# Turned blocks in fixed order, row power ahead of the weighted product, later transposes: one transformer block on one core

## The chip, the cores and the metric

The kernel runs on one core of a Trainium2 chip. A core has five engines that run side by side, each through its own queue in program order, and wait for each other through semaphores: TensorE (PE in the profile; its weight loads are PEld), VectorE (DVE), ScalarE (ACT), GpSimd (POOL) and SyncE (SP), which here only starts transfers. SBUF is the working memory of 128 partitions; PSUM holds what PE writes, in banks of 512 float32 per partition. The metric is the device time of one execution, in microseconds; lower is better.

## The reference

One block of depth 1 over 256 tokens of width 2048, all in float32: a feed-forward part, a mixer of two branches, and a second feed-forward part, each added to the running rows h after a norm of its own.

```python
def _rmsnorm(x, g):
    y = xf * lax.rsqrt(jnp.mean(xf * xf, axis=-1, keepdims=True) + NORM_EPS)
    return (y * g.astype(jnp.float32)).astype(x.dtype)

def _swiglu(x, w_gate, w_up, w_down):
    return (jax.nn.silu(x @ w_gate) * (x @ w_up)) @ w_down
...
f = _swiglu(_rmsnorm(h, ln_ffn1_pre[l]), ffn1_gate[l], ffn1_up[l], ffn1_down[l])
h = h + MACARON_WEIGHT * _rmsnorm(f, ln_ffn1_post[l])
mx = _hybrid_mixer(_rmsnorm(h, ln_mix_pre[l]), w_in[l], ...)
h = h + _rmsnorm(mx, ln_mix_post[l])
f = _swiglu(_rmsnorm(h, ln_ffn2_pre[l]), ffn2_gate[l], ffn2_up[l], ffn2_down[l])
h = h + MACARON_WEIGHT * _rmsnorm(f, ln_ffn2_post[l])
```

The hidden width of the feed-forward parts is 5632. The mixer projects to 8480 columns, runs a recurrence over 16 heads and a pooling branch, and ends with a 2048 x 2048 product. The change does not touch the mixer's inside.

## The kernel before

**Products in three.** Each float32 operand is cut in two: a rounded part (H, by a copy to the type fp32r) and what is left (L, by a subtraction). A product is three matmuls, H by H, H by L and L by H (`mm3`, lines 155 to 157; `mm` is the PSUM tile). Weights come as tiles of two k-steps of 128 rows by 512 columns (`get_w`, line 117, on SP's queue, into `w32`, four buffers). `two` casts a tile on ACT (line 131, `wH`, here called the cast) and subtracts on DVE (line 132, `wL`, the split); these pairs have five buffers. The 256 tokens are two halves, h = 0 and 1, of 128; a k-step of one half is three matmuls of 128x512.

**Turned blocks.** A product needs its left operand with the columns on the partitions. `transpose_split` (line 335) takes 128 tokens by 512 columns: PE transposes four pieces of 128x128 into one PSUM bank (line 339, tile `tr`). Where a norm stands ahead, its weights `gT` are multiplied in on the way: for each piece ACT writes scaled `xH` (line 345, the copy) and DVE scaled piece less `xH` (line 346, `xL`, the difference). These four pairs are called a block. The norm's other factor, one over the root of the row's mean square, is applied later, when the product leaves PSUM (`rs`).

**The head.** `head` writes the order of the first product by hand. x and the first gate weights are loaded in chunks, blocks are turned and tiles split, and PE runs k-steps of both halves as they come. `load(0, 0)` starts the first chunk of x on SP's queue; `load(None, None)` starts the norm weights' 16 rows of 128 (tile `g1rows`) and has PE turn and DVE copy them to `g1`. After the head, `stats` sums the squares of the rows (line 372, ACT, tile `junk`).

**The end of each part.** `post` multiplies by the down weights, 512 columns at a time (c = 0 to 3). For each half and c, when the product leaves PSUM, `sumsq` on ACT adds the squares (line 372, `ss`), and DVE multiplies the product by the post-norm weights (line 420, `fg`, here the product with the norm weights). At c = 2 the first three sums are gathered. After c = 3, `norm` makes the mean on DVE (line 439, tile `rt2`) and its power of -1/2 on POOL (line 441, the row power `r`); then `out` makes four row products on DVE (line 445: `fg` times `r` plus the residual), and `emit` stores each 512 columns on POOL's queue and has them turned for the next part. The last `post` stores the result through SP's queue instead and turns nothing.

**The order around the hand-over.** `run` keeps a clock of its own, `s.now`, in planned microseconds: items (k-steps of 3 x 0.2265) advance it, and events are recorded when it has reached their time. The last product (c = 3) runs its last 16 k-steps half by half (`by_half`): first all of half 0, then half 1. The next product begins by half too (`lead`, 10 k-steps of half 0, then 10 of half 1). When half h ends at `end`, the mean and power are recorded at `end` + 0.9, the four row products at `end` + 1.7, 2.4, 3.1 and 3.8, and the four turned blocks at `end` + `TURNS[h][q]` (line 44). Each turned block advances the clock by 0.45 (`TT`). So the blocks of half 0 stand among the last k-steps of half 1, and those of half 1 among the first k-steps of the next product. Two such hand-overs exist: from the first feed-forward part to the mixer, and from the mixer to the second feed-forward part. Casts and splits of the next product's tiles are events as well, 6.0 ahead of their k-steps (`AHEAD`). Within these stretches the order of PE, ACT and DVE is as recorded; elsewhere a scheduler of the framework orders the instructions by a plan of its own.

Of the kernel before, what the change touches and what calls it, by code (L numbers as in the profile page):

```python
# [14 lines left out]
ALU = mybir.AluOpType  # L15
# [25 lines left out]
STAG = 10  # L41
TRAIL = 16
AHEAD = (5.0, 6.0)
TURNS = [[3.6, 4.7, 5.8, 6.9], [3.6, 4.6, 5.6, 6.6]]
TB = 4

ROWS = [("ln_mix_pre", 16), ("ln_ffn2_pre", 16), ("mu", 26), ("w0", 8), ("a0", 8),
# [4 lines left out]
class Block:  # L52
# [154 lines left out]
    def head(s, w, c0, KT, do, keep, xs):  # L207

        load, turn = xs
        w32 = {}  # L210

        def get(k, n):
            w32[k] = (n, s.get_w(w, k, n, c0, 512, own=True))

        def split(k):
            n, t = w32[k]
            keep(s.two(t, k, n, 512))
        E = mybir.EngineType
        with s.tc.manual_schedule(engines={E.PE, E.Activation, E.DVE, E.SP}):
            load(0, 0)  # L220
            load(None, None)
            get(0, 1)
            get(1, 1)
            load(1, 0)
            get(2, 1)
            get(3, 1)
            for c in range(1, 4):
                load(0, c)
                get(4 * c, 2)
                load(1, c)  # L230
                get(4 * c + 2, 2)
            split(0)
            turn(0, 0)
            split(1)
            do(0, 0)
            turn(1, 0)
            split(2)
            do(1, 0)
            split(3)
            do(0, 1)  # L240
            do(1, 1)
            do(2, 0)
            do(2, 1)
            for c in range(4):
                k = 4 * c
                if c < 3:
                    turn(0, c + 1)
                    split(k + 4)
                if c:
                    for i in range(3):  # L250
                        do(k + i, 0)
                        do(k + i, 1)
                        if c < 3 and i == 1:
                            turn(1, c + 1)
                            split(k + 6)
                elif c < 3:
                    turn(1, c + 1)
                    split(k + 6)
                do(k + 3, 0)
                do(k + 3, 1)  # L260
            s.stats()
# [73 lines left out]
    def transpose_split(s, src, T, j, h, gT=None):  # L335
        nc = s.nc
        ps = s.psum("tr").rearrange("p (k t) -> p k t", k=4)
        for i in range(4):
            nc.tensor.transpose(ps[:, i], src[:, i * P:(i + 1) * P], s.ident)  # L339
        dH = T[j][0][:, :, h * P:h * P + P]  # L340
        dL = T[j][1][:, :, h * P:h * P + P]
        if gT is not None:
            for i in range(4):
                g = gT[:, j * 4 + i:j * 4 + i + 1]
                nc.scalar.activation(out=dH[:, i], in_=ps[:, i], func=AF.Copy, scale=g)  # L345
                nc.vector.scalar_tensor_tensor(out=dL[:, i], in0=ps[:, i], scalar=g,  # L346
                                               in1=dH[:, i].bitcast(F32), op0=ALU.mult,
                                               op1=ALU.subtract)
            return
        nc.scalar.copy(dH, ps)  # L350
        nc.vector.tensor_tensor(out=dL, in0=ps, in1=dH.bitcast(F32), op=ALU.subtract)

    def turn(s, T1, h, src):

        s.nc.vector.transpose(out=T1[:, h * 512:h * 512 + 512], in_=src)
# [46 lines left out]
    def post(s, wd, at, KT, gpost, fac, resid, emit, reload):  # L402
        nc = s.nc
        gb = [s.unit(p="gb") for _ in range(2)]
        fg = [[s.unit(p="fg") for _ in range(2)] for _ in range(2)]
        ss = [s.small(4, "ss") for _ in range(2)]

        def cc_(u, c):
            return u[c // 2][:, (c % 2) * 512:(c % 2) * 512 + 512]

        part = [None, None]
        kf = 1.0 / (D * fac ** 2)

        for c in range(4):
            def ev(h, ps):
                if h == 0 and c % 2 == 0:
                    nc.gpsimd.dma_start(out=gb[c // 2], in_=gpost[c * 512:c * 512 + 1024]  # L417
                                        .partition_broadcast(P))
                s.sumsq(ps, ss[h][:, c:c + 1])
                nc.vector.tensor_tensor(out=cc_(fg[h], c), in0=ps, in1=cc_(gb, c), op=ALU.mult)  # L420
                if c == 2 and h == 0:
                    reload()
                if c == 2:
                    p = s.small(1, "rt", bufs=2)
                    nc.vector.tensor_reduce(out=p, in_=ss[h][:, :3], axis=AX.X, op=ALU.add)
                    part[h] = s.small(1, "rp", bufs=2)
                    nc.vector.tensor_scalar(out=part[h], in0=p, scalar1=kf,
                                            scalar2=NORM_EPS / fac ** 2, op0=ALU.mult,
                                            op1=ALU.add)
                if c == 3:  # L430
                    end = s.now
                    r = s.small(1, "rs", bufs=8)
                    s.at(end + 0.9, lambda: norm(h, r))
                    for q in range(4):
                        s.at(end + 1.7 + 0.7 * q, lambda q=q: out(h, q, r, end))

            def norm(h, r):
                r2 = s.small(1, "rt2", bufs=2)
                nc.vector.tensor_scalar(out=r2, in0=ss[h][:, 3:4], scalar1=kf,
                                        scalar2=part[h], op0=ALU.mult, op1=ALU.add)  # L440
                nc.gpsimd.tensor_tensor(out=r, in0=r2, in1=s.mhalf[:, :1], op=ALU.pow)

            def out(h, q, r, end):
                o = cc_(fg[h], q)
                nc.vector.scalar_tensor_tensor(out=o, in0=o, scalar=r, in1=resid(h, q),  # L445
                                               op0=ALU.mult, op1=ALU.add)
                emit(h, q, o, end + TURNS[h][q])
            s.gemm_tok(wd, c * 512, at, KT, ev, trail=(c == 3))

    def next_pre(s, gT):  # L450
# [758 lines left out]
```

## Time and profile before

| | |
|---|---|
| median of 3 runs | 2136.59 us (2135.99 to 2136.96) |
| the profiled execution | 2136.39 us |
| its span, first to last instruction | 2134.7 us |
| mean granted TensorE clock | 0.993 |
| weights by SP's queue | 385.21 MB of 406.99 MB |
| mean rate of all transfers | 191 GB/s |

A span is what the profile covers; the time of an execution is a little longer. In rows of the profile an engine's name is followed by line, operation, the tile written, an arrow, and the tiles read. Sums count one of the engines alone; "[0.99 <-DVE fg]" behind a row is the time that the engine had idled just before, and what ended that idling. A matmul's duration includes its way through the array: those that follow each other start closer than a duration. PEclk is the share of the full clock that TensorE was granted.

### The profile page before, as it was taken

The page shows a single profiled execution, that of the slowest core. Times are in us where ns is not written, and L with a number is a line of the kernel's source. Part 1 is how long each engine was busy: PE and PEld are TensorE (multiplying, and loading weights), DVE is VectorE, ACT ScalarE, POOL GpSimd, SP SyncE. Part 2 cuts the span into 40 slices and gives each one's busy share as a digit, 9 for nine tenths or more (in the row PEclk, how much of TensorE's full clock was granted, in tenths as well). Part 3 has the DMA queues.
Part 4 walks back from the last instruction along what each step waited for, and adds up shares of the span by engine and source line. Part 5 has one row for each costly group of instructions (what it writes and reads, how often), then busy time and mean ns, then how long its engine had stood idle before and what let it go on. Part 6 is the DMA issues. An engine that isn't in the chain of part 4 may idle for free.

```text
span 2134.7 us, 28779 instructions
## 1 busy us (share of the span) xinstructions
PE 2099.6 (98%) x11077; PEld 1763.6 (83%) x11077; DVE 1261.6 (59%) x1588; ACT 1119.9 (52%) x1600; POOL 73.7 (3%) x161
## 2 busy tenths in 40 slices
PE   8999999999999999999999999989999999999998
PEld 6888888888888779989988788868888888888886
DVE  5555555565444465698789666565555555554444
ACT  6556555655444355465465444465665556554442
POOL 0000000000000000000210110000000000000000
PEclk9999999999999999999999999999999999999999
DMA  5665666667666556656546575556666665775654
GB/s 202 205 195 178 206 197 191 184 201 253 196 192 193 177 168 193 177 160 194 143 148 188 158 257 181 194 169 201 193 185 201 196 191 177 221 244 193 195 192 136
DMA packets 224116, 406.99 MB, mean 191 GB/s; under 512 B 13151, under 2 KB 49129, under 8 KB 223977
## 3 DMA queue, kind: packets, MB, share of 16 engines
q1 hardware_dynamic: 218089, 385.21, 58.7%
q0 software_dynamic: 5888, 19.93, 2.6%
q8 instruction: 87, 1.43, 0.3%
q14 instruction: 52, 0.43, 0.1%
HBM read 396.69 MB, written 8.39 MB: 190 GB/s over the span
## 4 chain that ended last, share of the span: by engine, by line
PE 95%; issue 2%; DVE 1%; ACT 1%; DMA 0%; POOL 0%; SPq 0%; DVEq 0%; POOLq 0%; ACTq 0%
PE mm L155 27%; PE mm L156 27%; PE mm L157 27%; PE mc L311 10%; PE tr L339 1%; DVE xL L346 0%; ACT xH L345 0%; PE pA L930 0%; ACT wH L131 0%; DVE wL L132 0%; PE pU L1026 0%; DVE fg L445 0%; PE pSa L1038 0%; PE pY L1061 0%; PE pY L1057 0%
## 5 line engine op out<-in xcount | busy, mean ns | idle before, releaser
L132 DVE TENSOR_TENSOR wL<-w,wH 128x1024 fp32r<-128x1024 f32 (+2 forms) x725 | 872.7, 1211 | 741.2 <-ACT wH L131 739.6
L131 ACT CAST wH<-w 128x1024 fp32r<-128x1024 f32 (+2 forms) x725 | 750.8, 1043 | 815.3 <-PE mm L157 673.0
L155 PE MATMUL mm<-wH,xH 128*128 128x512 f32 x2460 | 966.6, 393 | 8.3 <-ACT wH L131 7.8
L156 PE MATMUL mm<-wL,xH 128*128 128x512 f32 x2460 | 962.0, 391 | 5.7 <-DVE wL L132 5.7
L157 PE MATMUL mm<-wH,xL 128*128 128x512 f32 x2460 | 960.2, 391 | 0.0
L155 PEld LDWEIGHTS mm<-wH,xH 128*128 128x128 f32 x2460 | 463.8, 189 | 108.2 <-ACT wH L131 11.5
L156 PEld LDWEIGHTS mm<-wL,xH 128*128 128x128 f32 x2460 | 463.9, 189 | 103.1 <-DVE wL L132 8.8
L157 PEld LDWEIGHTS mm<-wH,xL 128*128 128x128 f32 x2460 | 463.8, 189 | 96.6
L311 PE MATMUL mc<-xH,wH 128*128 128x256 f32 x560 | 159.6, 285 | 0.0
L311 PE MATMUL mc<-xL,wH 128*128 128x256 f32 x560 | 158.4, 283 | 0.0
L311 PE MATMUL mc<-xH,wL 128*128 128x256 f32 x560 | 158.4, 283 | 0.0
L365 ACT COPY x<-T 32x256 f32<-32x256 f32 x352 | 141.9, 403 | 3.9
L311 PEld LDWEIGHTS mc<-xH,wH 128*128 128x128 f32 x560 | 105.9, 189 | 1.0
L311 PEld LDWEIGHTS mc<-xH,wL 128*128 128x128 f32 x560 | 106.0, 189 | 0.3
L311 PEld LDWEIGHTS mc<-xL,wH 128*128 128x128 f32 x560 | 106.0, 189 | 0.2
L345 ACT ACTIVATE xH<-tr,cols 128x128 fp32r<-128x128 f32 x64 | 22.6, 366 | 41.7 <-DVE xL L346 25.2
L384 ACT ACTIVATE sg<-mm,rs 128x512 f32<-128x512 f32 x44 | 30.1, 689 | 21.9 <-PE mm L157 21.9
L385 DVE SCALAR_TENSOR_TENSOR sg<-mm,rs,sg 128x512 f32<-128x512 f32 x44 | 31.7, 751 | 9.0 <-ACT sg L384 9.0
L372 ACT ACTIVATE junk<-mm 128x512 bf16<-128x512 f32 x24 | 14.3, 597 | 37.5 <-PE mm L157 37.5
L346 DVE SCALAR_TENSOR_TENSOR xL<-tr,cols,xH 128x128 fp32r<-128x128 f32 x64 | 22.0, 349 | 20.1 <-ACT xH L345 20.1
L417 POOL DMA_DIRECT2D gb<-in_ln_ffn_post_dram x4 | 2.4, 592 | 877.4 <-DVE xL L369 844.0
L420 DVE TENSOR_TENSOR fg<-mm,gb 128x512 f32<-128x512 f32 x24 | 16.5, 692 | 27.2 <-ACT junk L372 27.2
(243 smaller groups left out, 1110.4 us busy)
## 6 DMA issues: line engine op xcount, KB each, us to landing
w<-in_ffn_up_dram SPq DMA_DIRECT2D x176, 512.0 KB
w<-in_ffn_down_dram SPq DMA_DIRECT2D x176, 512.0 KB
w<-in_ffn_gate_dram SPq DMA_DIRECT2D x174, 512.0 KB
w<-in_w_in_dram SPq DMA_DIRECT2D x128, 512.0 KB
w<-in_w_out_dram SPq DMA_DIRECT2D x32, 512.0 KB
w<-in_w_proj_b_dram SPq DMA_DIRECT2D x16, 512.0 KB
w<-in_w_proj_a_dram SPq DMA_DIRECT2D x16, 512.0 KB
hsp<-fg POOLq DMA_DIRECT2D x16, 256.0 KB, 3.0
```

The lines of the kernel that those rows point to most:

```text
L131: s.nc.scalar.copy(vH, v)
L132: s.nc.vector.tensor_tensor(out=vL, in0=v, in1=vH.bitcast(F32), op=ALU.subtract)
L155: nc.tensor.matmul(ps, aH, bH, start=start, stop=False)
L156: nc.tensor.matmul(ps, aH, bL, start=False, stop=False)
L157: nc.tensor.matmul(ps, aL, bH, start=False, stop=stop)
L311: s.nc.tensor.matmul(o, lh, rh, start=one and n == 0, stop=k == KT - 1 and n == 2, skip_group_check=True)
L339: nc.tensor.transpose(ps[:, i], src[:, i * P:(i + 1) * P], s.ident)
L345: nc.scalar.activation(out=dH[:, i], in_=ps[:, i], func=AF.Copy, scale=g)
L346: nc.vector.scalar_tensor_tensor(out=dL[:, i], in0=ps[:, i], scalar=g, in1=dH[:, i].bitcast(F32), op0=ALU.mult, op1=ALU.subtract)
L365: nc.scalar.copy(dst[q * 32:q * 32 + 32, :, :, i], src[i * 32:i * 32 + 32, :, :, q])
L384: nc.scalar.activation(out=sg, in_=ps, func=AF.Sigmoid, scale=rs[h])
L385: nc.vector.scalar_tensor_tensor(out=sg, in0=ps, scalar=rs[h], in1=sg, op0=ALU.mult, op1=ALU.mult)
```

## The change

Four edits. In `transpose_split` the four copies of a block are recorded first and then the four differences. In `post` the product with the norm weights of c = 3 is recorded with the mean and the power, behind both. `TURNS` has later times. In the head, the transfer of the norm weights' rows is started ahead of the first chunk of x.

```diff
-TURNS = [[3.6, 4.7, 5.8, 6.9], [3.6, 4.6, 5.6, 6.6]]
+TURNS = [[4.2, 5.3, 6.4, 7.5], [4.0, 5.0, 6.2, 7.4]]
...
+            load(None, None)
             load(0, 0)
-            load(None, None)
             get(0, 1)
...
         if gT is not None:
-            for i in range(4):
-                g = gT[:, j * 4 + i:j * 4 + i + 1]
+            gs = [gT[:, j * 4 + i:j * 4 + i + 1] for i in range(4)]
+            for i, g in enumerate(gs):
                 nc.scalar.activation(out=dH[:, i], in_=ps[:, i], func=AF.Copy, scale=g)
+            for i, g in enumerate(gs):
                 nc.vector.scalar_tensor_tensor(out=dL[:, i], in0=ps[:, i], scalar=g,
                                                in1=dH[:, i].bitcast(F32), op0=ALU.mult,
                                                op1=ALU.subtract)
...
+                def scale():
+                    nc.vector.tensor_tensor(out=cc_(fg[h], c), in0=ps, in1=cc_(gb, c),
+                                            op=ALU.mult)
                 s.sumsq(ps, ss[h][:, c:c + 1])
-                nc.vector.tensor_tensor(out=cc_(fg[h], c), in0=ps, in1=cc_(gb, c), op=ALU.mult)
+                if c < 3:
+                    scale()
...
                     r = s.small(1, "rs", bufs=8)
-                    s.at(end + 0.9, lambda: norm(h, r))
+                    s.at(end + 0.9, lambda: (norm(h, r), scale()))
```

## The prediction

> **What bounds the kernel now.** I read the page first, then PE's waits, then windows around each wait, then the timelines in them. The page's busy times:
>
> ```profile
> PE 2099.6 (98%) x11077; PEld 1763.6 (83%) x11077; DVE 1261.6 (59%) x1588; ACT 1119.9 (52%) x1600; POOL 73.7 (3%) x161
> ```
>
> PE is busy nearly always, so only its waits, and time in which it runs slowly, can be won. The view of PE's waits (total us, times, longest) names whom it waits for:
>
> ```profile
> PE mm L155 <- ACT wH L131: 7.8, 9, 1.7
> PE tr L339 <- DVE fg L445: 5.8, 4, 1.9
> PE mm L156 <- DVE wL L132: 5.7, 8, 0.8
> ```
>
> By the timeline these sit in three stretches: the head, and the two hand-overs (down product to mixer, output product to second feed-forward). Windows (stretch, its length, busy us of PE, PEld, DVE, ACT, POOL with counts, PEclk, DMA share, GB/s):
>
> ```profile
> 17.05:42.24 25.19, 19.60 (x79) 14.00 (x77) 14.38 (x28) 14.14 (x30) 0.00 (x0) 0.93 0.35 130
> 42.24:66.00 23.76, 23.76 (x105) 19.64 (x106) 16.00 (x19) 18.14 (x30) 3.49 (x4) 1.00 0.75 230
> 734.71:763.75 29.04, 22.39 (x94) 16.61 (x93) 18.18 (x36) 13.39 (x31) 4.39 (x8) 0.82 0.48 159
> 1385.36:1414.74 29.38, 22.48 (x94) 16.97 (x92) 18.19 (x37) 13.73 (x32) 4.40 (x8) 0.83 0.48 162
> ```
>
> The second row is the undisturbed state: 105 matmuls in 23.76 us, 0.226 us each, clock 1.00. The other three have PE idle for 5.6 to 6.9 us, and a lower clock besides. What holds ACT and DVE there are the turned blocks:
>
> ```profile
> L345 ACT ACTIVATE xH<-tr,cols 128x128 fp32r<-128x128 f32 x64 | 22.6, 366 | 41.7 <-DVE xL L346 25.2
> L346 DVE SCALAR_TENSOR_TENSOR xL<-tr,cols,xH 128x128 fp32r<-128x128 f32 x64 | 22.0, 349 | 20.1 <-ACT xH L345 20.1
> ```
>
> Each copy waits for the difference before it, each difference for its copy. One period of the head (start, us, engine):
>
> ```profile
> 22.48 1.03 ACT L131 CAST wH<-w 128x1024 fp32r<-128x1024 f32 x1
> 23.41 0.37 ACT L345 ACTIVATE xH<-tr,g 128x128 fp32r<-128x128 f32 x1
> 23.55 1.22 DVE L132 TENSOR_TENSOR wL<-w,wH 128x1024 fp32r<-128x1024 f32 x1 [0.58 <-ACT wH L131]
> 25.07 0.37 ACT L345 ACTIVATE xH<-tr,g 128x128 fp32r<-128x128 f32 x1 [1.28 <-DVE xL L346]
> 25.86 0.37 ACT L345 ACTIVATE xH<-tr,g 128x128 fp32r<-128x128 f32 x1 [0.42 <-DVE xL L346]
> 26.91 1.04 ACT L131 CAST wH<-w 128x1024 fp32r<-128x1024 f32 x1
> ```
>
> Copies follow each other at 0.79 us, and cast to cast is 4.43 us. In that time PE has two k-steps for both halves (12 matmuls, 2.7 us) and one group of four transposes.
>
> **The change part by part.** *Copies, then differences.* The order of the built program shows that copies two to four of a block carry no wait, and differences two to four none; the first difference waits for the fourth copy. What such pieces take unhindered:
>
> ```profile
> 737.70 0.62 ACT L345 ACTIVATE xH<-tr,cols 128x128 fp32r<-128x128 f32 x2 [0.42 <-DVE xL L346]
> 770.31 0.60 DVE L346 SCALAR_TENSOR_TENSOR xL<-tr,cols,xH 128x128 fp32r<-128x128 f32 x2
> 40.20 3.88 ACT L131 CAST wH<-w 128x1024 fp32r<-128x1024 f32 x4
> 41.27 4.63 DVE L132 TENSOR_TENSOR wL<-w,wH 128x1024 fp32r<-128x1024 f32 x4 [0.58 <-ACT wH L131]
> 24.38 0.39 PE L157 MATMUL mm<-wH,xL 128*128 128x512 f32 x1
> 24.62 0.60 PE L339 MATMUL tr<-ident,x 128*128 128x128 f32 x4
> 25.28 0.39 PE L156 MATMUL mm<-wL,xH 128*128 128x512 f32 x1
> ```
>
> Two copies take 0.62, so one follows the other at 0.25 (0.62 less 0.37): four hold ACT for 1.02 and are done after 1.13. Differences: 0.26, four hold DVE 1.04. Casts follow at 0.95 (3.88 less 1.04, by three), splits at 1.13. A group of transposes adds 0.45 to PE (24.38 to 25.28 is 0.90, less two matmuls). A period then needs 1.97 of ACT, 2.17 of DVE, but 2.71 + 0.45 = 3.16 of PE: PE becomes the bound.
>
> *The first difference waits for the fourth copy.* That is the one lengthened wait: it comes 0.75 later than now, and the splits stand behind it on DVE. The sum contains it. The Trainium skill (PSUM — Partial Sum Buffer, PSUM bank collisions raise a hardware error) says that two engines must not touch one bank of the same partitions at a time, reads included, which agrees with the 25.2 us above; without that rule the first difference could follow the first copy, and the two hand-overs would gain up to 0.8 each more.
>
> *Head.* Early on, two waits of PE go, since the second tile's cast and split now finish by 7.5 and 8.3, ahead of PE:
>
> ```profile
> 8.85 0.79 PE L155 MATMUL mm<-wH,xH 128*128 128x512 f32 x1 [0.21 <-ACT wH L131]
> 9.57 0.29 PEld L156 LDWEIGHTS mm<-wL,xH 128*128 128x128 f32 x1 [0.44 <-DVE wL L132]
> 14.79 1.03 PE L339 MATMUL tr<-ident,x 128*128 128x128 f32 x8
> ```
>
> So what follows comes 0.65 sooner: the eight transposes at 14.1, the next four at 16.4 in place of 17.05. From there to 42.24, PE has k-steps 4 to 13 and the first matmul of the next, 61 matmuls, and four groups of transposes: 61 x 0.226 + 4 x 0.45 = 15.6. One wait is left: the copies of the block begin at 14.75 (0.63 after its transposes, as at the hand-over below), the last is done at 15.9, differences to 16.95, split to 18.2; PE, at 17.1 by then, waits 1.1. Later splits run ahead (2.17 against 3.16). Before 25.19, after 15.6 + 1.1 = 16.7, and 0.65 ahead: **-9.1**. The eight sums of squares follow among the next product's casts as now: 8 x 0.6 + 8 x 0.95 = 12.4 us of ACT against 96 matmuls, 21.7 us.
>
> *Norm rows' transfer first.* Row and wait:
>
> ```profile
> 1.25 0.42 SPq L1134 DMA_DIRECT2D g1rows<-in_ln_ffn_pre_dram  x1
> 7.52 0.71 PEld L339 LDWEIGHTS tr<-ident,x 128*128 128x128 f32 x4 [0.79 <-DMA x<-in_x_dram]
> ```
>
> The first chunk of x is issued 0.45 later, the weight tile behind both when it was. The chain passes the cast of that tile, and PE then waits 0.79 for the other half's chunk, which covers a shift. Bounds 0 to +0.45; I take 0, as the wait is the longer.
>
> *Turns later.* The planner's new times put each group of the first half one k-step (0.68) later, and spread those of the second half to one per k-step; the number of transposes is the same, so PE pays nothing. All four row products now stand ahead of the first differences on DVE. The rows of the first hand-over:
>
> ```profile
> 734.71 0.60 PE L339 MATMUL tr<-ident,fg 128*128 128x128 f32 x4
> 735.34 0.37 ACT L345 ACTIVATE xH<-tr,cols 128x128 fp32r<-128x128 f32 x1 [3.83 <-PE tr L339]
> 752.94 0.60 ACT L372 ACTIVATE junk<-mm 128x512 bf16<-128x512 f32 x1
> 756.88 1.12 PE L339 MATMUL tr<-ident,fg 128*128 128x128 f32 x4 [1.92 <-DVE fg L445]
> ```
>
> New times: groups at 735.39 and every 1.13 (0.68 + 0.45) to 738.78; six k-steps end the half at 743.3, six of the next product end at 747.4. ACT starts copies at 736.02 (0.63 after the transposes) and has, by the built order, four blocks and five casts ahead of the sum of squares: 4 x 1.02 + 5 x 0.95 = 8.8, so that starts at 744.85 in place of 752.94 and ends at 745.55. DVE starts differences at 737.15; four blocks and five splits, 4 x 1.04 + 5 x 1.13 = 9.8, to 747.0. Then the row power; what is late next is this, behind the splits. Its price is read at the end of the span, where nothing covers it:
>
> ```profile
> 2126.93 0.69 DVE L420 TENSOR_TENSOR fg<-mm,gb 128x512 f32<-128x512 f32 x1 [6.65 <-ACT junk L372]
> 2127.54 0.20 DVE L439 TENSOR_SCALAR rt<-ss,rp 128x1 f32<-128x1 f32 x1
> 2128.41 2.74 DVE L445 SCALAR_TENSOR_TENSOR fg<-fg,rs,h 128x512 f32<-128x512 f32 x4 [0.66 <-POOL rs L441]
> ```
>
> From the mean to the first row product 0.87, that product 0.75: transposes of the second half at 748.7, PE idle for 1.3. Four groups with a k-step each, 4.5, and the second half starts at 753.2. Before: 763.75. **-10.5**. The second hand-over has the same queues, 650.65 later: 1403.85 against 1414.74, **-10.9**. Nothing gives it back soon after: the second half's first differences are done by 750.8, for 753.2; four sums of squares (0.6 each) and the cast ahead of k-step 10 end by 757.1, its split by 758.8, for 760.0; DMA there moves 159 GB/s, against 230 in the undisturbed row.
>
> *Row power first.* The product with the norm weights (0.61 to the next row) leaves the chain, and is covered by the mean and the power (0.87). At the end of the span **-0.6** (0 if the cover fails); elsewhere it is in the times above. The new wait, the mean's for the sum of squares, is the product's old one, with the same work queued behind.
>
> **Sum.** 9.1 + 10.5 + 10.9 + 0.6 = 31.1 us. The profiled execution took 2136.39, 1.69 over its span of 2134.7, and lies 0.2 under the median: 2136.59 - 31.1 = **2105.5**.
>
> **Rivals.** *The slow clock stays.* Windows of 3.41 us:
>
> ```profile
> 17.11:20.52 3.41, 1.16 (x7) 0.61 (x6) 2.10 (x4) 1.83 (x4) 0.00 (x0) 1.00 1.05 386
> 20.52:23.93 3.41, 3.41 (x9) 2.64 (x10) 1.52 (x5) 2.30 (x5) 0.00 (x0) 0.50 1.05 386
> 737.32:740.73 3.41, 2.42 (x15) 1.80 (x14) 2.10 (x6) 1.36 (x4) 0.54 (x1) 1.00 0.16 59
> 747.56:750.97 3.41, 1.43 (x5) 0.86 (x5) 1.73 (x5) 1.86 (x4) 0.00 (x0) 1.00 0.53 146
> 750.97:761.21 10.24, 7.62 (x22) 5.62 (x23) 7.76 (x13) 4.38 (x10) 2.23 (x4) 0.50 0.68 227
> ```
>
> PE busy for 1.16 or 1.43 us of a window: half clock in the next. Busy for 2.42: none. My idles of 1.1 to 1.3 leave 2.1 to 2.3, nearer the latter. If they count, one window at half costs 1.7 us at three places, and 10.24 costs 5.1 at each hand-over: 2110.6 to 2117. The Trainium skill (TensorE: Matmul & The Clock Gate, Part 1: The HAM clock gate) gives a window of 3413 ns and half clock after an idle one; the lengths agree, but by its word an idle window would be needed and this rival would cost nothing, while here windows with 1.16 and 1.43 of work sufficed.
>
> *A wait for the fifth weight tile.* Four are buffered; the fifth is issued when the first is split, at 739.4, and cast, by my queue, at 743.9. If it lands 3 us later than that, beside the stores of the rows, the row power is 2.7 late and a slow window follows: 4.4 to 7.8 per hand-over, 2114 to 2121. Against it: in that stretch the queues moved 159 GB/s of at least 386 seen.
>
> *It does not do what it says:* copies still paced by differences, 2136. The built order speaks against it.
>
> *Slower.* Reads of the blocks do not pipeline when four stand together. Break-even where a period is again 4.43: copies at 0.87 apart (0.95 + 4 x 0.87). At 0.95 the head loses 0.32 in six periods, each hand-over 16 x 0.16: +7, 2143.6. The pair at 0.62 speaks against it.
>
> **How the numbers follow.** Forecast 0.70 (its own range 2101 to 2110: all three idles gone is -3.7, one slow window and a shifted start +2 to +4), clock 0.14, fifth tile 0.10, no effect 0.02, slower 0.04. The range 2100 to 2117 takes in the forecast, the clock and half of the fifth tile. 0.2% is 4.3 us, about what a measurement here can tell from no change: faster 0.94, within it 0.02, slower 0.04.
>
> **What would show it.** Right: no wait of a copy for a difference but on the first of a block; PE's waits for casts and splits down from 13.5 to about 1; PE at k-step 14 of the head near 33, the second half of the mixer's first product near 744 (753.2 less the head's 9.1), clock 1.00 throughout; the first row product at the end 0.87 after its mean, with the product in between. Wrong: blocks longer than 2.3 us, a wait for a transfer at the hand-overs, windows at 0.50, or new waits of PE for casts behind the sums of squares.

## The result, and the profile after

| | before | after |
|---|---|---|
| median | 2136.78 us (2135.99 to 2138.47, 4 runs) | 2106.53 us (2104.77 to 2107.15, 4 runs) |
| the profiled execution | 2136.39 | 2106.46 |
| its span | 2134.7 | 2104.8 |
| mean granted TensorE clock | 0.993 | 0.998 |

The ratio is 0.9856, with an interval of 0.9839 to 0.9873: 30.25 us faster, by the medians. The forecast was 2105.5 us, 2100 to 2117.

The page's busy times of the changed kernel, and PE's waits (total us, times, longest):

```profile
PE 2085.8 (99%) x11077; PEld 1758.1 (84%) x11077; DVE 1255.8 (60%) x1588; ACT 1116.2 (53%) x1600; POOL 73.5 (3%) x161
```

```profile
PE pg L1141 <- DMA g1rows<-in_ln_ffn_pre_dram: 2.6, 1, 2.6
PE tr L339 <- DVE fg L450: 2.3, 2, 1.2
PE tr L339 <- DMA x<-in_x_dram: 2.1, 1, 2.1
PE mc L311 <- DVE mxT L752: 1.8, 1, 1.8
...
PE mm L156 <- DVE wL L132: 0.9, 1, 0.9
```

The instruction counts are the same as before. The waits for casts and splits, 7.8 and 5.7 us in 17 places, are down to 0.9 in one; those for row products are down from 5.8 to 2.3. The wait for x is at the start and is new: before, PE waited there 4.0 for the norm rows alone, now 2.6 for them and then 2.1 for x. The turned blocks, by shape (busy, mean ns of one, idle before them and its cause):

```profile
L345 ACT ACTIVATE xH<-tr,cols 128x128 fp32r<-128x128 f32 x64 | 18.1, 391 | 16.7 <-PE tr L339 16.7
L347 DVE SCALAR_TENSOR_TENSOR xL<-tr,cols,xH 128x128 fp32r<-128x128 f32 x64 | 17.8, 345 | 4.0 <-ACT xH L345 4.0
```

Copies wait for transposes alone, no longer for differences (25.2 us before); the differences' waits for copies went from 20.1 to 4.0. One period of the head, rows picked from the timeline (start, us, engine; PE's products between the transposes are left out):

```profile
20.31 0.60 PE L339 MATMUL tr<-ident,x 128*128 128x128 f32 x4
20.74 1.22 DVE L132 TENSOR_TENSOR wL<-w,wH 128x1024 fp32r<-128x1024 f32 x1
20.94 1.15 ACT L345 ACTIVATE xH<-tr,g 128x128 fp32r<-128x128 f32 x4 [0.71 <-PE tr L339]
21.96 1.06 ACT L131 CAST wH<-w 128x1024 fp32r<-128x1024 f32 x1
22.12 1.13 DVE L347 SCALAR_TENSOR_TENSOR xL<-tr,g,xH 128x128 fp32r<-128x128 f32 x4 [0.16 <-ACT xH L345]
23.16 1.22 DVE L132 TENSOR_TENSOR wL<-w,wH 128x1024 fp32r<-128x1024 f32 x1
23.52 0.60 PE L339 MATMUL tr<-ident,x 128*128 128x128 f32 x4
```

Four copies take 1.15, four differences 1.13, and group follows group at 3.21 with PE never idle between them. ACT now waits for PE. The first hand-over, rows picked from the timelines of DVE, ACT and PE:

```profile
734.05 3.49 DVE L132 TENSOR_TENSOR wL<-w,wH 128x1024 fp32r<-128x1024 f32 x3
735.23 0.70 ACT L373 ACTIVATE junk<-mm 128x512 bf16<-128x512 f32 x1
737.45 0.21 DVE L444 TENSOR_SCALAR rt<-ss,rp 128x1 f32<-128x1 f32 x1
737.58 0.69 DVE L421 TENSOR_TENSOR fg<-mm,gb 128x512 f32<-128x512 f32 x1
738.35 2.74 DVE L450 SCALAR_TENSOR_TENSOR fg<-fg,rs,xr 128x512 f32<-128x512 f32 x4
739.16 0.66 PE L339 MATMUL tr<-ident,fg 128*128 128x128 f32 x4 [1.16 <-DVE fg L450]
```

The sum of squares is out of ACT at about 736, but the mean begins only at 737.45: it stands behind three splits. PE idles 1.16 for the first row product. And the end of the span, rows picked:

```profile
2096.44 0.39 PE L157 MATMUL mm<-kH,xL 128*128 128x512 f32 x1
2096.87 0.60 ACT L373 ACTIVATE junk<-mm 128x512 bf16<-128x512 f32 x1 [10.19 <-PE mm L157]
2097.59 0.21 DVE L444 TENSOR_SCALAR rt<-ss,rp 128x1 f32<-128x1 f32 x1 [7.24 <-ACT junk L373]
2097.72 0.68 DVE L421 TENSOR_TENSOR fg<-mm,gb 128x512 f32<-128x512 f32 x1
2098.47 2.74 DVE L450 SCALAR_TENSOR_TENSOR fg<-fg,rs,h 128x512 f32<-128x512 f32 x4
```

The first row product comes 0.88 after the mean, with the product in between.

Where the span's 29.9 us came from is read at four marks on PE: the first transposes of each hand-over (725.83 and 1367.47; before 734.71 and 1385.36, plus 0.68 for the k-step by which the turns moved), the start of the second half of the next product (743.73 and 1385.37; before 763.75 and 1414.74), the last matmul (2096.44; before 2125.79), and the end of the span.

| stretch | forecast | measured |
|---|---|---|
| head, to the first transposes of hand-over 1 | -9.1 | -9.56 |
| hand-over 1 | -10.5 | -10.46 |
| from there to hand-over 2 | 0 | +1.45 |
| hand-over 2 | -10.9 | -10.80 |
| from there to the last matmul | 0 | +0.02 |
| after the last matmul | -0.6 | -0.55 |
| sum | -31.1 | -29.90 |

The one stretch that is far from its forecast, +1.45, holds a window at half clock inside the mixer. Windows of the changed kernel (stretch, its length, busy us of PE, PEld, DVE, ACT, POOL with counts, PEclk, DMA share, GB/s):

```profile
915.80:919.21 3.41, 1.61 (x12) 1.32 (x11) 3.34 (x7) 1.33 (x3) 0.00 (x0) 1.00 0.36 132
919.21:922.63 3.42, 3.42 (x11) 2.83 (x12) 3.36 (x5) 1.59 (x4) 0.00 (x0) 0.50 0.33 103
```

Half of 3.41, 1.7 us, is lost there; the 0.25 by which the stretch lost less was not traced. PE had waited 1.8 for the mixer's `mxT` in the window before (fourth row of the waits above). The kernel before waits 1.7 there, and no half clock follows.

### The profile page after: what moved, and what is told of

Its sections match the earlier page's. It is cut to its first block, busy times and chain, and to the rows that moved or that the text cites. A ratio compares the mean times of both kernels' runs of the same rounds, so it can differ in the third digit from the quotient of the medians.

```text
span 2104.8 us, 28799 instructions
## 1 busy us (share of the span) xinstructions
PE 2085.8 (99%) x11077; PEld 1758.1 (84%) x11077; DVE 1255.8 (60%) x1588; ACT 1116.2 (53%) x1600; POOL 73.5 (3%) x161
## 4 chain that ended last, share of the span: by engine, by line
PE 90%; issue 8%; DVE 1%; DMA 0%; POOL 0%; ACT 0%; POOLq 0%; DVEq 0%; SPq 0%; ACTq 0%
PE mm L155 26%; PE mm L157 25%; PE mm L156 25%; PE mc L311 10%; PE pA L935 0%; PE tr L339 0%; DMA mb<-msp 0%; PE pU L1031 0%; PE pY L1066 0%; PE pSa L1043 0%; DVE fg L450 0%; PE pY L1062 0%; PE pM L1001 0%; PE pS L1051 0%; DMA x<-in_x_dram 0%
## 5 line engine op out<-in xcount | busy, mean ns | idle before, releaser
L385 ACT ACTIVATE sg<-mm,rs 128x512 f32<-128x512 f32 x44 | 29.9, 690 | 21.5 <-PE mm L157 21.5
L386 DVE SCALAR_TENSOR_TENSOR sg<-mm,rs,sg 128x512 f32<-128x512 f32 x44 | 31.5, 751 | 8.4 <-ACT sg L385 8.4
L356 DVE STREAM_TRANSPOSE T<-sg 128x512 f32<-128x512 f32 x44 | 30.9, 703 | 0.0
L391 DVE SCALAR_TENSOR_TENSOR sg<-mm,rs,sg 128x512 f32<-128x512 f32 x44 | 30.9, 745 | 0.0
L345 ACT ACTIVATE xH<-tr,cols 128x128 fp32r<-128x128 f32 x64 | 18.1, 391 | 16.7 <-PE tr L339 16.7
```

What stands on the lines that cost most here:

```text
L385: nc.scalar.activation(out=sg, in_=ps, func=AF.Sigmoid, scale=rs[h])
L386: nc.vector.scalar_tensor_tensor(out=sg, in0=ps, scalar=rs[h], in1=sg, op0=ALU.mult, op1=ALU.mult)
L391: nc.vector.scalar_tensor_tensor(out=sig[h], in0=ps, scalar=rs[h], in1=sig[h], op0=ALU.mult, op1=ALU.mult)
```

## The experiments

Each run is the kernel named with the edit shown. Times are medians. The kernel before, run beside them, had 2136.71 us for the first four rows, 2136.29 for the next four and 2137.07 for the last two.

| run | us | ratio to before, interval |
|---|---|---|
| copies_only | 2109.29 | 0.9872 (0.9857 to 0.9887) |
| no_copies | 2134.41 | 0.9989 (0.9980 to 0.9999) |
| turns_old | 2107.18 | 0.9862 (0.9847 to 0.9877) |
| pairs | 2118.74 | 0.9916 (0.9901 to 0.9931) |
| scale_old | 2107.22 | 0.9864 (0.9851 to 0.9878) |
| g1_back | 2106.62 | 0.9859 (0.9845 to 0.9872) |
| t2 | 2103.58 | 0.9845 (0.9832 to 0.9859) |
| best | 2101.16 | 0.9835 (0.9822 to 0.9849) |
| fifth_late | 2104.84 | 0.9848 (0.9834 to 0.9863) |
| after_again | 2106.95 | 0.9860 (0.9844 to 0.9877) |

**copies_only.** The kernel before with the first edit alone.

```diff
-            for i in range(4):
-                g = gT[:, j * 4 + i:j * 4 + i + 1]
+            gs = [gT[:, j * 4 + i:j * 4 + i + 1] for i in range(4)]
+            for i, g in enumerate(gs):
                 nc.scalar.activation(out=dH[:, i], in_=ps[:, i], func=AF.Copy, scale=g)
+            for i, g in enumerate(gs):
                 nc.vector.scalar_tensor_tensor(out=dL[:, i], in0=ps[:, i], scalar=g,
```

> The kernel before with one edit of the four: the copies of a block first, then its differences. Theory (the pace of the copies and differences is nearly the whole of the gain): head as in the changed kernel, hand-overs nearly so. Left out are 0.6 at the end (row power behind the product), and at each hand-over the old turns, where the fourth row product stands behind the first differences on DVE and PE's fourth transposes wait for it, about 1 us each. Gained back perhaps 0.65 at the start (x first). 2107 to 2112 us; no copy waits for a difference; PE's waits for row products 4 to 6 us in place of 2.3. Rival (the later turns and the early row power carry a good part, since they take the row products out of the queue behind the blocks): 2118 us or more, with the groups of transposes at the hand-overs waiting for row products for 10 us or more.

27.4 us of the 30.25 came with this edit alone. PE's waits in it:

```profile
PE tr L339 <- DVE fg L446: 4.7, 6, 1.4
...
PE mm L156 <- DVE wL L132: 0.9, 1, 0.9
```

The waits for casts and splits are gone as in the changed kernel, and no copy waits for a difference; those for row products are 2.4 us more, as the theory had it.

**no_copies.** The changed kernel with the old loop in `transpose_split`.

```diff
-            for i, g in enumerate(gs):
+            for i in range(4):
+                g = gT[:, j * 4 + i:j * 4 + i + 1]
                 nc.scalar.activation(out=dH[:, i], in_=ps[:, i], func=AF.Copy, scale=g)
-            for i, g in enumerate(gs):
                 nc.vector.scalar_tensor_tensor(out=dL[:, i], in0=ps[:, i], scalar=g,
```

> The changed kernel with copies and differences interleaved again as before; later turns, row power first and norm rows first are kept. Theory: the three other edits are worth 0.6 at the end and nothing else that counts: 2134 to 2137 us, copies of a block 0.79 apart, cast to cast 4.4 in the head, PE's waits for casts and splits 12 to 14 us, windows at half clock at both hand-overs. Rival (the turns carry a part): 2120 to 2130 us, with the second half of the mixer's first product more than 3 us sooner after the head than in the kernel before.

2.3 us of gain are left by the medians, inside the range that was expected, but not for the reason given there (0.6 at the end and nothing else that counts). By the marks, the span is 2.95 shorter than before: 0.89 and 1.65 are won at the two hand-overs, 0.59 at the end and 0.26 between the hand-overs, and 0.43 is lost at the start. ACT at the first hand-over:

```profile
736.45 0.37 ACT L345 ACTIVATE xH<-tr,cols 128x128 fp32r<-128x128 f32 x1 [4.51 <-PE tr L339]
737.24 0.37 ACT L345 ACTIVATE xH<-tr,cols 128x128 fp32r<-128x128 f32 x1 [0.42 <-DVE xL L346]
```

and PE's waits:

```profile
PE mm L155 <- ACT wH L131: 12.1, 7, 4.4
PE mm L156 <- DVE wL L132: 5.5, 9, 0.8
PE tr L339 <- DVE fg L449: 2.7, 2, 1.3
```

Copies are 0.79 apart again, and three windows at half clock follow at each hand-over, as in the kernel before. The waits for casts and splits are 17.6, more than the 12 to 14 expected: the row products are less in the way (2.7 where before had 5.8), and PE waits for the third cast instead, 4.4 at each hand-over. With the later turns two blocks stand ahead of that cast on ACT; it starts at 750.56, and at 750.11 before. The two halves of the change add up: 27.4 + 2.3 = 29.7, for 30.25 measured.

**pairs.** The changed kernel with one return from DVE to ACT in the middle of a block.

```diff
+            for p in (0, 2):
+                for i in (p, p + 1):
+                    nc.scalar.activation(out=dH[:, i], in_=ps[:, i], func=AF.Copy, scale=gs[i])
+                for i in (p, p + 1):
+                    nc.vector.scalar_tensor_tensor(out=dL[:, i], in0=ps[:, i], scalar=gs[i],
+                                                   in1=dH[:, i].bitcast(F32), op0=ALU.mult,
+                                                   op1=ALU.subtract)
```

> The changed kernel with each block as two copies, two differences, two copies, two differences: one change of engine in the middle of a block, where the kernel before has three and the changed kernel none. Theory (the cost is the round trip between ACT and DVE at each change of engine, with the cast and the split behind it): a period of ACT and DVE becomes about 3.35 us (before 4.43, changed 2.17), just over PE's 3.16 in the head: about 1 us there. At each hand-over four periods stand ahead of the sum of squares: 4 x (3.35 - 2.17) = 4.7 us. Together 10 us: 2114 to 2120 us. Rival (PE is the bound once a block is under some pace, the hand-overs included): 2106 to 2109 us.

The runs fell at 2116.5 to 2116.7 and 2120.8 to 2121.1. ACT at the first hand-over, whose first transposes are at 728.26 in this run:

```profile
730.72 1.05 ACT L131 CAST wH<-w 128x1024 fp32r<-128x1024 f32 x1
...
734.10 1.05 ACT L131 CAST wH<-w 128x1024 fp32r<-128x1024 f32 x1
...
742.13 0.60 ACT L374 ACTIVATE junk<-mm 128x512 bf16<-128x512 f32 x1
```

Cast to cast is 3.38 (3.35 expected), with one block between the two, and the sum of squares starts 13.87 after the first transposes, against 9.40 in the changed kernel: 4.47 later (4.7 expected). The time of a period thus falls with the number of returns from DVE to ACT within a block: 4.43 with three, 3.38 with one, 2.17 (the splits' distance on DVE in the changed kernel) with none. It does not fall in proportion: the first two returns taken away save 1.05 together, the last one 1.21. In the head PE's own 3.21 hides most of the last step, but not at a hand-over, where four periods stand ahead of the sum of squares. The rival falls. The time of the whole run measures this less well than the periods do. The first transposes of the hand-over come 2.4 later than in the changed kernel, where the theory had 1 for the head. And this profiled run has four windows at half clock, three of them at the hand-overs, which the theory did not count, at 1.7 each. Why the two groups of times lie 4.3 apart was not traced.

**turns_old.** The changed kernel with the old times of the turns.

```diff
-TURNS = [[4.2, 5.3, 6.4, 7.5], [4.0, 5.0, 6.2, 7.4]]
+TURNS = [[3.6, 4.7, 5.8, 6.9], [3.6, 4.6, 5.6, 6.6]]
```

> The changed kernel with the old times of the turns. Theory: the row power comes up to 0.7 sooner at each hand-over, as the blocks of the first half are handed out one k-step sooner; but the fourth row product stands behind the first differences, and PE waits for it, about 0.4 in the first half and 1.0 in the second: 0 to 1.5 us slower over both hand-overs, 2106 to 2109 us, PE with four or more waits for row products in place of two. Rival (the later turns are what lets the hand-overs run): 5 us slower or more, 2111 us or above.

```profile
PE tr L339 <- DVE fg L450: 3.5, 6, 0.8
```

Six waits for row products in place of two, as expected, yet by the median it is 0.65 slower only. The marks say more: from the first transposes to the second half's start it takes 19.58 (725.38 to 744.96), with one k-step more between them than the changed kernel's 17.90: 19.58 - 0.68 - 17.90 = 1.0 lost at this hand-over, and as much at the second (1366.41 to 1386.01, 19.60). None of its windows in the mixer was at half clock, which gives 1.7 back against the profile of the changed kernel. One part of the theory fell: the row power was not sooner. ACT's queue has two blocks ahead of the first cast there, and the fifth weight tile comes late:

```profile
728.17 1.06 ACT L131 CAST wH<-w 128x1024 fp32r<-128x1024 f32 x1
...
734.99 1.05 ACT L131 CAST wH<-w 128x1024 fp32r<-128x1024 f32 x1 [0.85 <-DMA w<-in_w_in_dram]
```

Its transfer starts at 731.18, when the first split has freed a buffer, and lands 3.8 later. In the changed kernel it starts at 729.92; the same 3.8 would end at 733.7, and the cast that needs it begins at about 734.3. The cover is 0.6 us by this estimate. copies_only, with the old turns too, waits 1.15 at this place.

**scale_old.** The changed kernel with the product ahead of the mean again.

```diff
                 s.sumsq(ps, ss[h][:, c:c + 1])
-                if c < 3:
-                    scale()
+                scale()
...
-                    s.at(end + 0.9, lambda: (norm(h, r), scale()))
+                    s.at(end + 0.9, lambda: norm(h, r))
```

> The changed kernel with the product with the norm weights of the last 512 columns ahead of the mean again. Theory: the product's 0.6 comes back onto the chain from the sum of squares to the first row product at the end and at both hand-overs, where PE's idle of 1.16 grows by it: 1.8 to 2.1 us slower, 2108 to 2109 us, PE's two waits for row products 3.5 us in all in place of 2.3. Rival (only the end counts, as the prediction's sum had it: the hand-overs are covered): 0.6 slower, 2107.1 us, waits as they are.

```profile
PE tr L339 <- DVE fg L449: 3.5, 2, 1.8
```

The two waits grew by 0.6 each, and the time from the last matmul to the end is 8.9 (2096.61 to 2105.5) where the changed kernel has 8.36: 0.5 to 0.6 in three places, 1.7 together. By its time alone, 0.7 slower, the run fits the rival (2107.1) and misses the theory (2108 to 2109); the waits decide, and the rival falls. This profiled run too had no half clock in the mixer. Beside the profile of after_again, which had none either, its span is 2.2 longer (2105.5 for 2103.3), of which 0.4 lies in the head (first transposes at 726.42 for 725.99).

**g1_back.** The changed kernel with x first again.

```diff
-            load(None, None)
             load(0, 0)
+            load(None, None)
```

> The changed kernel with the first chunk of x started ahead of the norm rows again. Theory (the price of the norm rows first is 0.65 at the start, and most of it passes down the head, since PE's later waits in the head are for its own pace): first transposes at 4.2 in place of 4.9, the next eight 0.5 to 0.7 sooner than 13.55, the kernel 0.5 to 0.7 faster: 2105.8 to 2106.1 us. Rival (the prediction's: it is covered by the wait for the other half's chunk): the eight transposes at 13.55 as now, 2106.5 us.

Inconclusive in time. With the norm rows first, PE's first transposes began between 4.72 and 5.15 in seven profiled runs; with x first between 4.09 and 4.32 in five. The price at that point is 0.73 between the means, 4.97 and 4.23. But the next eight transposes came at 13.26 in place of 13.55, and in other runs of the same two orders of the start with the same blocks at 13.70, 13.78, 13.90 and 14.13 against 13.21, 13.66 and 13.23: the means, 13.81 and 13.34, are 0.5 apart, the spread within an order is as large.

**t2 and best.** The idles that are left, taken away: the order of g1_back, the turns of the second half of the rows two k-steps later (t2), and besides that the first whole tile's cast and split ahead of the second block of the head, where ACT is idle (best).

```diff
-TURNS = [[4.2, 5.3, 6.4, 7.5], [4.0, 5.0, 6.2, 7.4]]
+TURNS = [[4.2, 5.3, 6.4, 7.5], [5.4, 6.5, 7.6, 8.7]]
...
-            load(None, None)
             load(0, 0)
+            load(None, None)
...
+                if c == 0:
+                    split(4)
                 if c < 3:
                     turn(0, c + 1)
-                    split(k + 4)
+                    if c:
+                        split(k + 4)
```

> The changed kernel with the first chunk of x first, and with the turns of the second half of the rows two k-steps (1.36) later. Theory: PE's idle of 1.16 at each hand-over goes, since it has two more k-steps to run while the row power and the first row product come; 0.6 from the start: 2.9 us faster, 2103.6 us, at most 0.3 given back at each hand-over if the second half then waits for its first difference: 2103.3 to 2104.5 us, no wait of PE for a row product. Rival (the chain of blocks, differences and second half is tight, so the later blocks delay the second half by what was won): 2105.5 to 2106.5 us, with PE waits for the turned block in place of those for the row product.

> The same with one step more: in the head the cast and split of the tile for k-steps 4 and 5 are recorded ahead of the second block instead of behind it. ACT is idle there for 2.7 us, so that they cost the block nothing if the tile has landed. Theory: PE's wait of 0.86 for that split goes: 2102.7 us (2102.4 to 2103.7). Rival (the tile lands late and holds up the block behind it in ACT's queue): 2104 us or more, with a wait of ACT for this weight transfer.

2103.58 and 2101.16 us. PE's waits in best:

```profile
PE pg L1144 <- DMA g1rows<-in_ln_ffn_pre_dram: 3.9, 1, 3.9
PE mc L314 <- DVE mxT L755: 1.8, 1, 1.8
PE pS L1054 <- ACT R L1048: 0.9, 1, 0.9
PE mm L155 <- ACT xH L348: 0.6, 1, 0.6
```

No wait for a row product, a cast or a split is left; what remains is the start and the mixer's inside. best came out 1.2 below the bottom of what was expected. Two reasons can be read from the traces. An idle of 0.86 in the waits view costs more than 0.86: it is counted from the modelled end of the matmul before it. From one matmul to the next it is 17.67 - 16.31 = 1.36 in the changed kernel, 1.13 over the usual 0.23. The other is the clock. The two spans are 3.3 apart (2102.1 and 2098.8): 1.7 up to the first transposes of the first hand-over (725.96 and 724.23), and 1.6 from there to those of the second (1366.22 and 1362.91), where t2's profile has a window at half clock in the mixer (918.42 to 921.83) and best's has none. That part is not the edit's. Of the first 1.7, 0.4 was there by the eight transposes (13.66 and 13.23); it may be the landing of the first weight tile, for which PE waited 1.2 in t2's profile (through the copies behind its cast) and 0.6 in best's.

**fifth_late.** The changed kernel with the fifth tile's cast and split recorded behind the second row product.

```diff
-                s.at(start + (k - k0) * 3 * MM - ahead,
+                s.at(start + (k - k0) * 3 * MM - ahead + (5.0 if k == 8 and k1 == STAG else 0.0),
```

> The changed kernel with one move: at each hand-over the cast and the split of the next product's fifth weight tile are recorded behind the second row product of the second half of the rows, not ahead of the mean. Theory (the mean of the second half stands on DVE behind the splits, which is what makes PE idle 1.16 at each hand-over): with one cast and one split fewer ahead, mean and row power come 1.1 us sooner, PE's wait for the first row product goes or falls under 0.2, the third may cost 0.2: 1.6 to 2.3 us less waiting of PE in all, 2104 to 2105.5 us where the median of the changed kernel stands at 2106.5. Rival (the mean waits for the sum of squares, which waits for PE, not for the splits): the first transposes of the second half stay 13.3 us behind the first ones of the first half, no gain, or a loss by a wait of PE for the fifth tile.

```profile
734.39 2.35 DVE L132 TENSOR_TENSOR wL<-w,wH 128x1024 fp32r<-128x1024 f32 x2
736.65 0.21 DVE L444 TENSOR_SCALAR rt<-ss,rp 128x1 f32<-128x1 f32 x1
736.78 0.68 DVE L421 TENSOR_TENSOR fg<-mm,gb 128x512 f32<-128x512 f32 x1
737.54 1.42 DVE L450 SCALAR_TENSOR_TENSOR fg<-fg,rs,xr 128x512 f32<-128x512 f32 x2
```

The mean follows its splits at once, one split sooner. The transposes of the second half come 12.19 after those of the first (726.16 to 738.35), not 13.33, and PE has no wait for a row product in its list. So it was the splits on DVE that the row power stood behind. 2104.84 us, 1.7 below the changed kernel's first runs and 2.1 below after_again beside it. The runs themselves overlap (2103.53 to 2105.29, and from 2104.77 on), so the marks show this better than the time does.

**after_again.** The changed kernel unchanged.

> The changed kernel once more, for its times and for the clock. Theory (the clock is decided in windows of 3.41 us on a grid that starts anew in each run; a window with PE busy for about 1.6 or less is followed by one at half clock): the runs fall in two groups 1.7 us apart, near 2104.8 and near 2106.6; in the profiled run the only place that can drop under 1.6 is PE's wait of 1.8 in the mixer, and the clock is half after it if, and only if, that wait lies whole inside one window. Rival (the one window at half clock was chance, or tied to that place): one group of times, or a window at half clock with PE busy for 2 us or more in the window ahead of it.

Its runs were 2105.01, 2106.6, 2107.3 and 2107.61; those of the changed kernel above 2104.77, 2106.46, 2106.6 and 2107.15. Two groups, as expected, the upper one 1.6 to 2.6 us above the lower, wider than the theory had it; only two of the eight runs are in the lower. The profiled run is of the lower group. Its mixer wait ended at 919.16, after 1.79, and lies across a border of the grid:

```profile
917.70:921.11 3.41, 1.95 (x11) 1.71 (x11) 3.30 (x6) 1.17 (x2) 0.00 (x0) 1.00 0.00 0
921.11:924.53 3.42, 3.42 (x21) 2.90 (x20) 3.42 (x5) 1.85 (x5) 0.00 (x0) 1.00 0.70 194
```

PE is busy for 1.95 in the one window, and the clock stays. The strict form of the theory fell by scale_old: there the wait lay whole inside a window and the clock stayed.

```profile
916.88:920.30 3.42, 1.62 (x12) 1.34 (x10) 3.35 (x7) 1.41 (x3) 0.00 (x0) 1.00 0.36 129
920.30:923.71 3.41, 3.41 (x22) 3.00 (x23) 3.35 (x5) 2.56 (x6) 0.00 (x0) 1.00 0.32 115
```

The same wait, with PE busy for 1.61 to 1.63 of its window, was followed by half clock in the changed kernel, fifth_late, pairs and t2, and at 1.62 not in scale_old: it lies on the border.

## Why the prediction was right or wrong

*Pace of copies and differences: right.* By the step four copies are done after 1.13, and the four differences hold DVE for 1.04. From the first's start to the last's end the trace has 1.15 and 1.13 (the last difference's own time is longer than the distance to the next), and splits 2.17 apart at the first hand-over (728.68 to 730.85), the very 2.17 of the step. PE's period is 3.21, the step had 3.16. That this is what the change is worth is shown from both sides, by copies_only and no_copies, and its dose by pairs.

*First difference behind the fourth copy: right.* In the period above it begins at 22.12, the fourth copy ends at 22.09. The rule of the Trainium skill (PSUM — Partial Sum Buffer, PSUM bank collisions raise a hardware error) agrees with that. But the wait itself stands in the order of the program, and no run left it out or spread a block over two banks, so what the rule costs here stays an estimate.

*Head: right in the sum (-9.56 for -9.1), in part by luck.* Two misses nearly cancel. The first matmul came 0.67 later than before (6.48 for 5.81), not at the same time; from there to the eight transposes 1.91 was won, not 0.65, so that they came 1.24 sooner. The two early waits went, as the step had it. What it had not was the clock: the distance from matmul to matmul fell from 0.43 to 0.23 at 11.5 in this run and at 13.9 before. By these figures the 2.4 us between are worth about 1.1, an estimate, which is most of the second miss. In the twelve profiled runs the full clock first came between 9.25 and 13.69, and the kernel before, the latest, was profiled once: how much of that is owed to the waits that went and how much to where the windows lay stays open. In the other runs of the changed head the eight came at 13.70, 13.78, 13.90 and 14.13, so the step's 14.1 is at the late end of the spread, and some 0.3 of the gain are this run's. K-step 14, forecast near 33, began at 32.87. The wait at k-step 4 came where the step put it, 1.13 lost for 1.1.

*Norm rows' transfer first: the bounds were wrong.* The step had 0 to +0.45 and took 0, as the weight tile's issue does not move. Its issue did not (1.71 for 1.72), but its cast began at 5.54 in place of 4.71: the tile was awaited 0.8 longer. In all seven profiled runs with this order the cast began between 5.37 and 5.78, in four of the five with x first between 4.58 and 4.94 (in t2 at 5.64). So the issue time did not bound the landing time here. PE's first transposes are 0.73 later with this order; of that nothing could be told in the medians.

*First hand-over: right, mark by mark.* Forecast less the head's 9.56: sum of squares 735.29 (735.23), mean 737.44 (737.45), transposes 739.14 (739.16), second half 743.64 (743.73). That the row power would be what is late next, behind the splits, is shown by fifth_late. *Second hand-over: right* (-10.80 for -10.9).

*Row power first: right,* 0.55 at the end; scale_old shows the same 0.6 at both hand-overs, where the step had it inside its marks.

*Turns later: the step booked nothing of their own.* They are worth 1.0 at each hand-over (turns_old), of which, at the first, part is the fifth tile: with the old turns it is waited for, 0.85 and 1.15. The rival of the fifth tile thus had the right place: by the estimate above the tile lands 0.6 ahead of its cast in the changed kernel, where the rival needed it 3 behind.

*The slow clock: right at the hand-overs, wrong for the whole.* The idles of 1.16 left PE 2.27 and more of a window, and no half clock followed there in the two profiled runs of the changed kernel. But "clock 1.00 throughout" was wrong by one window, from a wait that the change does not touch. That 1.45, less 0.46 won over the forecast in the head, is most of the 1.2 between the sum, 31.1, and the span's 29.9. Without that window the changed kernel takes 2105.01, in after_again's profiled run, and probably 2104.77, in a run that has only its mean clock of 0.999 to show for it, for a forecast of 2105.5. The 0.46 won over the forecast in the head hides part of that miss in the median, which lies 1.0 above the forecast; that is luck.

## What to carry to other kernels

Where two engines take turns on one small buffer, count the returns from one to the other, not the instructions: four and four cost 2.17 a period here, the same eight in turn 4.43, and the price shows two queues further on, as PE waiting for weights. After such a wait is gone, look for what stands ahead of the next short chain on its engine (here a mean of 128 numbers behind three splits), and move that work, or give PE more to do meanwhile. And compare small edits by marks and waits in the traces, since one window of half clock, 1.7 us, hid most of what the later turns are worth: 2.0 us by the marks, 0.65 by the medians.

## What the runs showed of the hardware

The clock is granted by windows of 3.41 us on a grid that lay differently from run to run (the start of the grid, read from the last drop of the clock, was between 0.04 and 3.20 us of the span). How long PE was busy in a window at full clock, and what the next one got, over the profiled runs of before, after and the experiments (the windows at the very end of the span are left out):

```
next at half clock:  0.00  0.95  1.04  1.12  1.17  1.43  1.43  1.61  1.61  1.62  1.63
next at full clock:  1.62  1.66  1.72  1.79  1.83  1.91  1.93  1.93  1.95  1.95  1.97  1.99  and all above
```

The border is near 1.62 of 3.41, a little under half, as the profile counts PE's busy time. From half clock, windows with 1.06 to 2.72 us of work were followed by another at half, those with 3.24 to 3.41 by full clock, so one gap cost the kernel before 10.24 us of half clock at a hand-over. The Trainium skill (TensorE: Matmul & The Clock Gate, Part 1: The HAM clock gate) says that the window is free-running and does not start with the kernel, which these traces agree with; that the half clock comes after an idle window falls short of what they show: the window with 0.00 was followed by it, but so were windows with 0.95 to 1.63 us of work.

A second thing: the time of the same wait in a list of waits and on the clock differ, 0.86 against 1.13. The list counts from the end of the matmul before it as the profile models it (16.31 + 0.49 = 16.80, to 17.67); without a wait the next matmul starts 0.23 after that one's start, not 0.49.
